# T products among the gate projections, and a state recurrence done by sums, a scan of every fourth step and an expansion

## The chip, the core and the metric

The kernel runs on one core of a Trainium2 chip. The metric is device time in microseconds of one execution, lower is better. The core has five engines with instruction streams of their own: TensorE (PE in the rows, PEld for its weight loads), VectorE (DVE), ScalarE (ACT), GpSimd (POOL) and SyncE (SP), which here issues nearly all DMAs.

## What is computed

Two transformer-like blocks on 512 tokens of width 1024. The first (two attentions, a cross attention and an MLP) is untouched. The second begins with the "even mixer", and the change lies in its S5 part, a bidirectional complex linear recurrence over 256 context and 512 latent tokens:

```python
lam_bar = jnp.exp(lam * step)
b_bar = ((lam_bar - 1.0) / lam)[..., None] * lax.complex(b_re, b_im)
bu = lax.complex(einsum('btgh,gph->btgp', u, b_bar.real), einsum('btgh,gph->btgp', u, b_bar.imag))
_, s = lax.associative_scan(_linear_recurrence, (a, bu), axis=1)      # s[t] = lam_bar * s[t-1] + bu[t]
return einsum('btgp,ghp->btgh', s.real, c_re) - einsum('btgp,ghp->btgh', s.imag, c_im)
```

with 48 groups of 16 channels and 64 states, forward and backward; `y = yf + yb + d * u`. Beside it, the mixer has a Fourier branch (256 channels), a gate projection `z`, a GLU and an output projection.

## The kernel before

**S5 in chunks.** Tokens are taken in chunks of eight, 32 context and 64 latent ones. `U[o]` (three tiles, 16 groups each) holds the inputs chunk by chunk. Three products on TensorE use them:
- the *state inputs*: 24 group pairs `gp`, each 8 products of `win` (fetched from the table `WinD` in DRAM, two pairs per tile) with `U` (L1209), evacuated into `St`, 128 partitions x 96 chunks x 2 directions x re/im x 24 pairs (L1213 on VectorE for odd pairs under 16, L1215 on ScalarE for the rest);
- the *T products*: what a chunk gives itself. `T` is fetched from `WD` by 8 DMAs a tile (L1263), the product of `T` and `U` (L1319) goes into `YC[o]`;
- the *E products*: `St` times `E` (fetched from `ED`, L1335; products L1343), added to `YC` by VectorE (L1348).

Between the first and the last, VectorE runs the recurrence over the 96 chunks: `tree` (L1184 to L1197) composes the first 32 chunks, the context, into one state by five levels of doubling, first for pairs 0 to 15, then for 16 to 23. The scan then goes chunk by chunk from 32 to 95, eight instructions a step on 128x48 elements (L1231 to L1237; four operations, two directions). The E products need the whole of it.

**What else runs there.** TensorE in the meantime does, in this order, the Fourier branch's input projection (`gemm_tok`, tiles `ub`), the gate projection `z` in four column groups of 256 (`gemm_ch`, 48 products of 128x512 each; the groups are called z3, z0, z1, z2 in the order in which they run), the transform (`k_dft`, then eight products with `fw`, result `yf`) and the Fourier part of the output projection (`even_out` below, 48 products of 128x512). Each matrix is used as a high and a low part: `wload` fetches `raw` (L131), ScalarE rounds it to `whi` (L137), VectorE subtracts to get `wlo` (L138, two instructions of 128x1024 for a z group). `mm3` (L175 to L177) issues hi x hi, lo x hi, hi x lo, so a group can't go on without its `wlo`. `raw`, `whi` and `wlo` have two buffers each.

**What sets the order.** Each engine runs its instructions in the order that the tile framework fixed when the program was built: it takes the instructions as written, with the place in the code as priority and its own model of their times, and gives buffers of the pools (`t4`: 12 of 4 KB, `big`: 9 of 8 KB, two PSUM banks `sc`, three `mm`) as they come free. `behind(n)` lowers a priority; the scan stands under `behind(3000)`. `self.step()`, called in the gemm helpers after the weights of a column group have been asked for, moves a generator in `self.sides` on; `self.after(n, f)` runs `f` after `n` flushes (one for each output tile). A matmul of type f32 (state inputs, T, E, `fw`) shows as two records in the trace.

Of the kernel before, what the change touches and what calls it, by code (L numbers as in the profile page):

```python
# [12 lines left out]
F32 = mybir.dt.float32  # L13
F32R = mybir.dt.float32r
AF = mybir.ActivationFunctionType
# [68 lines left out]
class Net:  # L84
# [8 lines left out]
    def setup(self):  # L93
        ctx, tc, nc, A = self.ctx, self.tc, self.nc, self.A
        P = lambda name, bufs, **k: ctx.enter_context(tc.tile_pool(name=name, bufs=bufs, **k))
        self.const = P("const", 1)
        self.sm = P("sm", 8)
        self.wp = P("wp", 2)
        self.t4 = P("t4", 12)
        self.big = P("big", 9)  # L100
        self.ps = P("ps", 1, space=PSUM)
        self.dram = P("dram", 1, space=bass.MemoryType.DRAM)
        self.ident = self.const.tile([128, 128], F32, name="ident")
        make_identity(nc, self.ident)
        self.mhalf = self.const.tile([128, 1], F32, name="mhalf")
        nc.vector.memset(self.mhalf, -0.5)
        self.sides = []
        self.late = []
# [795 lines left out]
    def s5_tables(self):  # L904

        nc, A = self.nc, self.A
        V = nc.vector
# [7 lines left out]
        ap = A["s5_log_step_2"]  # L915
# [40 lines left out]
        p = self.trp()  # L956
# [9 lines left out]
        t = self.ptile("pow")  # L966
# [24 lines left out]
        self.s5P = self.t4k("s5P")[:, :576].rearrange("p (j r n) -> p j r n", j=4, r=3)  # L991
        re, im = sw[:, 0], sw[:, 1]
        x = t[:, :48]
        for j in range(4):
# [170 lines left out]
    def even(self, hT, U, vpool):  # L1165
        nc, A = self.nc, self.A
        V = nc.vector
# [11 lines left out]
        def tree(g0, gn):  # L1179

            mt = [self.t4k("tree"), self.t4k("tree")]
            for lev in range(5):
                h = 1 << lev
                n = 16 // h  # L1184
                for d in range(2):
                    m1, m2 = mt[d][:, :4 * n * gn].rearrange("p (k m r g) -> k p m r g", k=2, m=n, r=2)
                    to = lambda t: t.to_broadcast([128, n, 2, gn])
                    if lev:
                        P3 = self.s5P[:, lev - 1, :, d * 24 + g0:d * 24 + g0 + gn]
                        a, b = to(P3[:, None, 0:1]), to(P3[:, None, 1:3])  # L1190
                    else:
                        a, b = [to(t[:, None, d, :, g0:g0 + gn]) for t in (self.s5A, self.s5B)]
                    dst = steps(d, 2 * h - 1, 2 * h, n, g0, gn, False)
                    V.tensor_mul(m1, a, steps(d, h - 1, 2 * h, n, g0, gn, False))
                    V.tensor_mul(m2, b, steps(d, h - 1, 2 * h, n, g0, gn, True))
                    V.tensor_add(m1, m1, dst)
                    V.tensor_add(dst, m1, m2)  # L1197

        for gp in range(24):
            o, l = divmod(gp, 8)  # L1200
            if gp % 2 == 0:
                win = self.t4k("win").rearrange("p (j d r n) -> p j d r n", j=2, d=2, r=2)
                nc.sync.dma_start(win, self.WinD[:, gp:gp + 2])
            p = self.bank("sc", 2)[:, :384].rearrange("p (r n) -> p r n", r=4)
            for d in range(2):
                for r in range(2):
                    for g in range(2):
                        u = 64 * (g ^ gp % 2)
                        nc.tensor.matmul(p[u:u + 64, 2 * d + r], win[:, gp % 2, d, r, 64 * g:64 * g + 64],  # L1209
                                         U[o][:, 8 * g + l, 32 * d:32 * d + 96], start=True, stop=True)  # L1210
            dst = St[:, :, :, :, gp].rearrange("p s d r -> p (d r) s")
            if gp % 2 and gp < 16:
                V.tensor_copy(dst, p)  # L1213
            else:
                nc.scalar.activation(dst, p, AF.Copy)  # L1215
        tree(0, 16)
        tree(16, 8)

        def at(d, j, swap=False):

# [4 lines left out]


        mt = self.const.tile([128, 192], F32, name="scan").rearrange("p (d m r g) -> d m p r g", d=2, m=2, r=2)
        with self.behind(3000):
            for j in range(32, 96):
                for d in range(2):  # L1230
                    V.tensor_mul(mt[d][0], self.s5A[:, d], at(d, j - 1))  # L1231
                for d in range(2):
                    V.tensor_mul(mt[d][1], self.s5B[:, d], at(d, j - 1, swap=True))  # L1233
                for d in range(2):
                    V.tensor_add(mt[d][0], mt[d][0], at(d, j))  # L1235
                for d in range(2):
                    V.tensor_add(at(d, j), mt[d][0], mt[d][1])  # L1237


        sz = [self.b8("sz", (128, 4, 512)) for _ in range(2)]  # L1240
# [16 lines left out]
        Ts = []  # L1257
        for o in range(3):
            T = self.b8("T", (128, 16, 128))
            for k in range(8):  # L1260
                src = bass.AP(tensor=self.WD.tensor, offset=self.WD.offset + o * 16 * 3840 + (7 - k) * 16,
                              ap=[[240, 16], [3840, 16], [1, 128]])
                nc.sync.dma_start(T[k * 16:(k + 1) * 16], src)  # L1263
            Ts.append(T)
# [17 lines left out]
        pq = []  # L1282
        for a, b in ((0, 258), (258, 514)):
            wh, wl = self.wload(A["k_dft"], 4, (a, b))
            t = self.t4k("pq")[:, :2 * (b - a)].rearrange("p (m n) -> p m n", m=2)
# [22 lines left out]
            self.split(*self.nat(t, yf[0][:, m], yf[1][:, m]))  # L1308


        YCs = []
        for o, T in enumerate(Ts):
            YCs.append(self.t4k("YC").rearrange("p (k l h) -> p k l h", k=8, h=16))
            for l0 in (0, 4):
                p = self.bank("sc", 2).rearrange("p (l n) -> p l n", l=4)
                for l in range(4):
                    for g in range(2):
                        k = 8 * g + l0 + l
                        nc.tensor.matmul(p[64 * g:64 * g + 64, l], U[o][:, k, 32:96], T[:, k], start=True, stop=True)  # L1319
                nc.scalar.activation(YCs[o][:, :, l0:l0 + 4].rearrange("p k l h -> p l k h"),  # L1320
                                     p.rearrange("p l (k h) -> p l k h", h=16), AF.Copy)

        gate = self.row(self.adaD[0, 2 * D:3 * D], self.t4k("gate"))

        self.gemm_tok([(yf[0][:, m], yf[1][:, m]) for m in range(2)], A["even_w_out_2"][0][768:], cols(0, D, 512), self.gated(gate))


        ga = []
        for o in range(3):
            YC = YCs[o]  # L1330
            for l0 in (0, 4):

                ps = [b[:, :256].rearrange("p (l n) -> p l n", l=2) for b in (self.bank("sc", 2), self.mm())]
                E = self.b8("E", (128, 4, 2, 2, 128))
                nc.sync.dma_start(E, self.ED[:, o * 8 + l0:o * 8 + l0 + 4])  # L1335
                for j0 in (0, 2):
                    for d in range(2):
                        s0 = 1 if d else 31
                        for r in range(2):
                            for j in (j0, j0 + 1):  # L1340
                                for g in range(2):
                                    q = slice(64 * (g ^ j % 2), 64 * (g ^ j % 2) + 64)
                                    nc.tensor.matmul(ps[j % 2][64 * g:64 * g + 64, j // 2], St[q, s0:s0 + 64, d, r, o * 8 + l0 + j], E[q, j, d, r],  # L1343
                                                     start=(d == 0 and r == 0), stop=(d == 1 and r == 1),
                                                     tile_position=(q.start, 64 * g), skip_group_check=True)
                for b, q in enumerate(ps):
                    dst = YC[:, :, l0 + b:l0 + 4:2].rearrange("p k l h -> p l k h")
                    V.tensor_add(dst, q.rearrange("p l (k h) -> p l k h", h=16), dst)  # L1348
# [171 lines left out]
```

## Time and profile before

| | |
|---|---|
| median of 3 runs | 1365.91 us (1364.2 to 1366.62) |
| the profiled execution | 1367.87 us, span from first to last instruction 1366.1 us |
| busy: PE, DVE, ACT, POOL | 95%, 72%, 41%, 5% |
| mean granted TensorE clock | 0.987 of full speed |
| DMA | 178.07 MB, mean 130 GB/s |

How to read it: times in the trace are microseconds from the span's start. A timeline row gives start, length, engine, line, operation, out<-in, shape, and in square brackets the idle time just before with what ended it. Instructions of an engine overlap at their ends, so what one costs in a row of them is the distance from start to start, not its length. The even mixer's S5 part, from the first state input to the GLU, runs from 969.5 to 1111.4 us.

### The profile page before, as it was taken

The page shows a single profiled execution, that of the slowest core. Times are in us where ns is not written, and L with a number is a line of the kernel's source. Part 1 is how long each engine was busy: PE and PEld are TensorE (multiplying, and loading weights), DVE is VectorE, ACT ScalarE, POOL GpSimd, SP SyncE. Part 2 cuts the span into 40 slices and gives each one's busy share as a digit, 9 for nine tenths or more (in the row PEclk, how much of TensorE's full clock was granted, in tenths as well). Part 3 has the DMA queues.
Part 4 walks back from the last instruction along what each step waited for, and adds up shares of the span by engine and source line. Part 5 has one row for each costly group of instructions (what it writes and reads, how often), then busy time and mean ns, then how long its engine had stood idle before and what let it go on. Part 6 is the DMA issues. An engine that isn't in the chain of part 4 may idle for free. (4 is left out here: it accounts for less than half of the span.)

```text
span 1366.1 us, 21191 instructions
## 1 busy us (share of the span) xinstructions
PE 1300.5 (95%) x8106; PEld 1081.4 (79%) x8106; DVE 987.5 (72%) x2284; ACT 557.6 (41%) x992; POOL 71.6 (5%) x135
## 2 busy tenths in 40 slices
PE   6999999999999999999999999979999789999997
PEld 5999577678888888787887887778888578787886
DVE  6998897868966464897999955683499966623545
ACT  5533643654526243433433433552433254333222
POOL 2000000021100010000000001010000000200000
PEclk9999999999999999999999999999999999999999
DMA  6422001155852236534777754541316934321321
GB/s 211 124 66 90 25 8 62 31 180 162 276 202 94 93 77 172 186 108 157 205 208 210 225 192 139 185 140 61 109 54 77 283 105 162 104 93 62 125 91 62
DMA packets 151877, 178.07 MB, mean 130 GB/s; under 512 B 27124, under 2 KB 118490, under 8 KB 151008
## 3 DMA queue, kind: packets, MB, share of 16 engines
q1 hardware_dynamic: 148560, 168.17, 40.6%
q0 software_dynamic: 3216, 8.56, 2.0%
q8 instruction: 64, 1.05, 0.3%
q14 instruction: 37, 0.30, 0.1%
HBM read 161.24 MB, written 15.45 MB: 129 GB/s over the span
## 5 line engine op out<-in xcount | busy, mean ns | idle before, releaser
L137 ACT ACTIVATE whi<-raw 128x1024 fp32r<-128x1024 f32 (+2 forms) x197 | 198.5, 1026 | 286.5 <-PE mm L176 114.3
L138 DVE TENSOR_TENSOR wlo<-raw,whi 128x1024 fp32r<-128x1024 f32 (+2 forms) x197 | 229.6, 1182 | 117.8 <-ACT whi L137 115.4
L175 PE MATMUL mm<-hmh,whi 128*128 128x512 f32 (+1 forms) x288 | 106.4, 369 | 0.0
L176 PE MATMUL mm<-hml,whi 128*128 128x512 f32 (+1 forms) x288 | 105.4, 366 | 0.0
L177 PE MATMUL mm<-hmh,wlo 128*128 128x512 f32 (+1 forms) x288 | 105.3, 366 | 0.0
L175 PE MATMUL mm<-whi,ah 128*128 128x512 f32 x256 | 101.8, 399 | 3.3 <-DVE x L620 3.3
L177 PE MATMUL mm<-whi,al 128*128 128x512 f32 x256 | 100.1, 394 | 0.2
L176 PE MATMUL mm<-wlo,ah 128*128 128x512 f32 x256 | 100.1, 393 | 0.0
L175 PE MATMUL mm<-whi,hTh 128*128 128x256 f32 (+1 forms) x304 | 88.5, 291 | 3.4 <-ACT whi L137 2.7
L176 PE MATMUL mm<-wlo,hTh 128*128 128x256 f32 (+1 forms) x304 | 86.9, 286 | 0.0
L177 PE MATMUL mm<-whi,hTl 128*128 128x256 f32 (+1 forms) x304 | 86.9, 286 | 0.0
L620 DVE TENSOR_TENSOR x<-mm,x 128x512 f32<-128x512 f32 x87 | 58.7, 685 | 32.6 <-PE mm L177 32.3
L781 DVE SCALAR_TENSOR_TENSOR adas<-adaw,cond,adas 128x1024 f32<-128x1024 f32 x56 | 70.6, 1277 | 10.2 <-DMA adaw<-ada_w_dram 10.0
L175 PE MATMUL mm<-h2h,whi 128*128 128x512 f32 x160 | 62.8, 392 | 0.0
L175 PEld LDWEIGHTS mm<-whi,ah 128*128 128x128 f32 x256 | 48.3, 189 | 18.1 <-DVE x L620 5.6
L175 PEld LDWEIGHTS mm<-whi,hTh 128*128 128x128 f32 x304 | 58.8, 193 | 4.4 <-ACT whi L137 3.1
L177 PE MATMUL mm<-h2h,wlo 128*128 128x512 f32 x160 | 62.3, 389 | 0.0
L176 PE MATMUL mm<-h2l,whi 128*128 128x512 f32 x160 | 62.3, 389 | 0.0
L175 PEld LDWEIGHTS mm<-hmh,whi 128*128 128x128 f32 x288 | 54.3, 189 | 9.6 <-issue 1.0
L177 PEld LDWEIGHTS mm<-hmh,wlo 128*128 128x128 f32 x288 | 54.3, 189 | 8.8
L176 PEld LDWEIGHTS mm<-hml,whi 128*128 128x128 f32 x288 | 54.4, 189 | 8.4
L176 PEld LDWEIGHTS mm<-wlo,hTh 128*128 128x128 f32 x304 | 58.5, 193 | 1.4 <-issue 1.3
(515 smaller groups left out, 3296.5 us busy)
## 6 DMA issues: line engine op xcount, KB each, us to landing
adaw<-ada_w_dram SPq DMA_DIRECT2D x48, 512.0 KB
raw<-w_up_dram SPq DMA_DIRECT2D x16, 1024.0 KB
raw<-w_down_dram SPq DMA_DIRECT2D x16, 1024.0 KB
raw<-odd_w_in_dram SPq DMA_DIRECT2D x12, 1024.0 KB
raw<-w_in_dram SPq DMA_DIRECT2D x11, 1024.0 KB
raw<-w_kv_cross_dram SPq DMA_DIRECT2D x8, 1024.0 KB
raw<-even_w_in_dram SPq DMA_DIRECT2D x8, 1024.0 KB
WinD<-wst SPq DMA_DIRECT2D x24, 256.0 KB
```

The costliest lines, as they stand in the source:

```text
L137: nc.scalar.activation(hi[:, k], raw[:, k], AF.Copy)
L138: nc.vector.tensor_sub(lo[:, k], raw[:, k], hi[:, k].bitcast(F32))
L175: nc.tensor.matmul(out, lh, rh, start=(first and i == 0), stop=False)
L176: nc.tensor.matmul(out, lh, rl, start=False, stop=False)
L177: nc.tensor.matmul(out, ll, rh, start=False, stop=(final and i == n - 1))
L620: self.nc.vector.tensor_add(self.x[i][:, c:c + n], p, self.x[i][:, c:c + n])
L781: nc.vector.scalar_tensor_tensor(acc[v], w, cond[:, v, k:k + 1], acc[v], op0=OP.mult, op1=OP.add)
```

## The change

- The state inputs' tiles `win` are fetched up to four ahead; evacuations all go to ScalarE; the products take banks of `sc` and `mm` in turn.
- The recurrence is done in other steps. `join(lev, j0, n, ...)` does one level: chunk j0, j0+2h, ... gets the state of h chunks before it. `join(0, 1, 48)` (384 elements an instruction) runs after every four pairs, `join(1, 3, 24)` (384 elements) after every eight, over all 96 chunks. The scan goes over every fourth chunk, 7 to 95, with the fourth power of lambda. Then chunks 33, 37, ... (`join(1, 33, 16)`, 256 elements) and 32, 34, ... (`join(0, 32, 32)`, 512 elements) are expanded for 8 pairs at a time.
- Scan and expansion are a generator in `self.sides`, moved on by `self.step()`; `behind(3000)` is gone. A `step` is added in the transform.
- T tiles 0 and 1 are fetched right after the tables, T2 within the scan; their products run by `self.after` among the projections. The six `E` tiles are fetched earlier: three at the scan's end, three after z.
- `s5P` (powers) goes from four levels in `t4` to two in `const`; `t4` has 13 buffers; the DMA scratch is set to 8192.

```diff
+        jt = [self.t4k("join") for _ in range(2)]
+        def join(lev, j0, n, g0, gn):
+            h = 1 << lev
+            for d in range(2):
+                m1, m2 = jt[d][:, :4 * n * gn].rearrange("p (k m r g) -> k p m r g", k=2, m=n, r=2)
...
+                dst = steps(d, j0, 2 * h, n, g0, gn, False)
+                V.tensor_mul(m1, a, steps(d, j0 - h, 2 * h, n, g0, gn, False))
+                V.tensor_mul(m2, b, steps(d, j0 - h, 2 * h, n, g0, gn, True))
+                V.tensor_add(m1, m1, dst)
+                V.tensor_add(dst, m1, m2)
...
+                while len(wins) < min(gp // 2 + 4, 12):
+                    wins.append(self.t4k("win").rearrange("p (j d r n) -> p j d r n", j=2, d=2, r=2))
...
-            if gp % 2 and gp < 16:
-                V.tensor_copy(dst, p)
-            else:
-                nc.scalar.activation(dst, p, AF.Copy)
-        tree(0, 16)
-        tree(16, 8)
+            nc.scalar.activation(dst, p, AF.Copy)
+
+            if gp % 4 == 3:
+                join(0, 1, 48, gp - 3, 4)
+            if l == 7:
+                join(1, 3, 24, gp - 7, 8)
+        Ts += [t_load(o) for o in range(2)]
+        for o in range(3):
+            self.after(2 + 3 * o, lambda o=o: t_part(o))
...
-        with self.behind(3000):
-            for j in range(32, 96):
+        def scan():
+            for j in range(7, 96, 4):
                 for d in range(2):
-                    V.tensor_mul(mt[d][0], self.s5A[:, d], at(d, j - 1))
+                    V.tensor_mul(mt[d][0], A4[d][:, 0:1].to_broadcast([128, 2, 24]), at(d, j - 4))
...
+                if j == 39:
+                    Ts.append(t_load(2))
+                if j == 95:
+                    Es.extend(e_load(n) for n in range(3))
+                if j % 28 == 11:
+                    yield
+            for g0 in (0, 8, 16):
+                join(1, 33, 16, g0, 8)
+                join(0, 32, 32, g0, 8)
+                yield
+        self.sides.append(scan())
```

How the fixed orders change, at three places. VectorE, where the low part of z1's weights is made. Before (`wlo_10454` is z1's, two halves of it):

```order
L1237 TENSOR_TENSOR St<-scan 128x48 x2
L1231 TENSOR_TENSOR scan<-s5A,St 128x48 x2
L1233 TENSOR_TENSOR scan<-s5B,St 128x48 x2
L138 TENSOR_TENSOR wlo_10454<-raw_10452,whi_10453 128x1024
L1235 TENSOR_TENSOR scan<-scan,St 128x48 x2
L1237 TENSOR_TENSOR St<-scan 128x48
L138 TENSOR_TENSOR wlo_10454<-raw_10452,whi_10453 128x1024
L1237 TENSOR_TENSOR St<-scan 128x48
L1231 TENSOR_TENSOR scan<-s5A,St 128x48 x2
```

and in the changed kernel (`wlo_10140` is z1's, `wlo_10262` z2's, `wlo_10360` the transform's):

```order
L1193 TENSOR_TENSOR join_9333<-s5A,St 128x512
L1196 TENSOR_TENSOR St<-join_9334 128x16x2x8
L1194 TENSOR_TENSOR join_9333<-s5B,St 128x512
L1195 TENSOR_TENSOR join_9333<-join_9333,St 128x512
L1193 TENSOR_TENSOR join_9334<-s5A,St 128x512
L1196 TENSOR_TENSOR St<-join_9333 128x32x2x8
L1194 TENSOR_TENSOR join_9334<-s5B,St 128x512
L1195 TENSOR_TENSOR join_9334<-join_9334,St 128x512
L1196 TENSOR_TENSOR St<-join_9334 128x32x2x8
L138 TENSOR_TENSOR wlo_10140<-raw_10138,whi_10139 128x1024 x2
L138 TENSOR_TENSOR wlo_10262<-raw_10260,whi_10261 128x1024 x2
L138 TENSOR_TENSOR wlo_10360<-raw_10358,whi_10359 128x774
```

The split of z1's weights stood in the middle of the scan; now it stands behind the last instruction of the expansion. In the same stream, the split of z0 (`wlo_10003`) stands behind the 9th of the 23 scan steps and the four `ub` splits, that of z3 ahead of the first join.

TensorE, end of z0 and begin of z1 in the changed kernel (`mm_10091` is z0's last tile, `sc_10117` and `sc_10127` the T2 products, `mm_10208` and `mm_10234` z1's first two tiles):

```order
L176 MATMUL mm_10091<-hll_8439,whi_10002 128x512
L177 MATMUL mm_10091<-hlh_8438,wlo_10003 128x512
L1223 MATMUL sc_10117<-T_9919,U_8656 64x128 x8
L1223 MATMUL sc_10127<-T_9919,U_8656 64x128 x8
L175 MATMUL mm_10208<-hlh_8436,whi_10139 128x512
L176 MATMUL mm_10208<-hll_8437,whi_10139 128x512
L175 MATMUL mm_10234<-hlh_8436,whi_10139 128x512
L176 MATMUL mm_10234<-hll_8437,whi_10139 128x512
L177 MATMUL mm_10208<-hlh_8436,wlo_10140 128x512
```

The T products, which stood in the output projection, now stand in the input projection, in z0 and between z0 and z1; the fifth product of z1 needs `wlo_10140`.

SyncE in the changed kernel (`raw_10138` and `raw_10260` are z1's and z2's weights):

```order
L1232 DMA win_9565<-WinD 128x1024
L1203 DMA T_9671<-WD 16x16x128 x3
L1203 DMA T_9680<-WD 16x16x128 x8
L1203 DMA T_9919<-WD 16x16x128 x8
L131 DMA raw_10138<-even_w_in_dram 128x8x256
L1208 DMA E_10202<-ED 128x2048
L1208 DMA E_10204<-ED 128x2048
L1208 DMA E_10206<-ED 128x2048
L131 DMA raw_10260<-even_w_in_dram 128x8x256
```

Before, both came ahead of all T and E tiles. Now z1's are queued behind the T tiles, and z2's behind the first three E tiles.

## Rows read from the trace of the kernel before

**Rows 1.** The page's head and its busy times.
```profile
span 1366.1 us, 21191 instructions
PE 1300.5 (95%) x8106; PEld 1081.4 (79%) x8106; DVE 987.5 (72%) x2284; ACT 557.6 (41%) x992; POOL 71.6 (5%) x135
```
**Rows 2.** Stretches: length, busy PE, PEld, DVE, ACT, POOL; PEclk, DMA share, GB/s.
```profile
1003.60:1047.30 43.70, 43.70 (x196) 36.19 (x195) 43.70 (x304) 12.94 (x19) 3.04 (x6) 1.00 0.27 72
1061.40:1090.60 29.20, 22.11 (x176) 18.18 (x176) 28.80 (x159) 6.39 (x12) 0.00 (x0) 0.88 1.11 293
```
**Rows 3.** Timeline of PE: last product of `ub`, first of z3, first after z2.
```profile
1003.61 0.28 PE L177 MATMUL mm<-whi,hll 128*128 128x256 f32 x1
1003.73 0.40 PE L175 MATMUL mm<-hlh,whi 128*128 128x512 f32 x1
...
1047.28 1.05 PE L1277 MATMUL tr<-fw 128*128 128x128 f32 x8
```
**Rows 4.** Timeline of PE from the transform to the E products: the idle times.
```profile
1052.31 0.38 PE L176 MATMUL mm<-wlo,ub 128*128 128x256 f32 x1 [0.98 <-DVE wlo L138]
...
1061.45 0.50 PE L175 MATMUL mm<-whi,yf 128*128 128x512 f32 x1 [2.66 <-ACT yf L309]
...
1067.39 3.76 PE L1319 MATMUL sc<-T,U 128*64 128x128 f32 x64
1076.37 3.32 PE L1319 MATMUL sc<-T,U 128*64 128x128 f32 x32 [5.22 <-DMA raw<-even_w_out_dram]
1080.81 2.06 PE L1343 MATMUL sc<-E,St 64*64 64x128 f32 x32 [1.12 <-DVE St L1237]
...
1090.60 1.73 PE L1343 MATMUL mm<-E,St 64*64 64x128 f32 x26
```
**Rows 5.** Timeline of PE and of ACT in the E products.
```profile
1097.15 0.40 PE L1343 MATMUL sc<-E,St 64*64 64x128 f32 x2 [1.07 <-issue]
...
1110.32 1.11 PE L1356 MATMUL tr<-ident,YC 128*128 128x128 f32 x4 [3.69 <-ACT ga L1357]
...
1108.72 1.06 ACT L137 ACTIVATE whi<-raw 128x1024 fp32r<-128x1024 f32 x1 [6.25 <-DMA raw<-odd_w_in_dram]
```
**Rows 6.** Timeline of DVE in the tree: 512 and 256 elements, start to start.
```profile
986.41 0.69 DVE L1194 TENSOR_TENSOR tree<-s5A,St 128x512 f32<-128x512 f32 x1
987.02 0.69 DVE L1195 TENSOR_TENSOR tree<-s5B,St 128x512 f32<-128x512 f32 x1
...
998.45 0.41 DVE L1194 TENSOR_TENSOR tree<-s5A,St 128x256 f32<-128x256 f32 x1
998.78 0.41 DVE L1197 TENSOR_TENSOR St<-tree 128x256 f32<-128x256 f32 x1
```
**Rows 7.** Timeline of DVE in the scan: the first operation of two steps.
```profile
1076.91 0.33 DVE L1231 TENSOR_TENSOR scan<-s5A,St 128x48 f32<-128x48 f32 x2
...
1077.87 0.33 DVE L1231 TENSOR_TENSOR scan<-s5A,St 128x48 f32<-128x48 f32 x2
```
**Rows 8.** Timeline of DVE: a weight split, a split of ub, a weight split.
```profile
1005.82 1.22 DVE L138 TENSOR_TENSOR wlo<-raw,whi 128x1024 fp32r<-128x1024 f32 x1
1006.96 0.42 DVE L310 TENSOR_TENSOR ub<-ubf,ub 128x256 fp32r<-128x256 f32 x1
1007.29 1.22 DVE L138 TENSOR_TENSOR wlo<-raw,whi 128x1024 fp32r<-128x1024 f32 x1
```
**Rows 9.** Timeline of ACT and DVE: evacuations of state inputs.
```profile
973.11 0.87 ACT L1215 ACTIVATE St<-sc 128x384 f32<-128x384 f32 x1
...
989.15 4.59 ACT L1215 ACTIVATE St<-sc 128x384 f32<-128x384 f32 x5 [0.16 <-PE sc L1209]
...
976.51 0.82 DVE L1213 COPY St<-sc 128x384 f32<-128x384 f32 x1 [0.98 <-PE sc L1209]
```
**Rows 10.** Timeline of PE after an idle time: first and fourteenth product.
```profile
912.46 0.55 PE L175 MATMUL mm<-whi,cxh 128*128 128x256 f32 x1 [6.47 <-DVE UC L815]
...
915.36 0.28 PE L176 MATMUL mm<-wlo,cxh 128*128 128x256 f32 x1
```

More of the change, by code (lines that the diff above doesn't have):

```diff
@@ L98, in setup @@
         self.wp = P("wp", 2)
-        self.t4 = P("t4", 12)
+        self.t4 = P("t4", 13)
         self.big = P("big", 9)
@@ L989, in s5_tables @@
         V.tensor_copy(self.s5B[:, :, 1], l8[:, 1])
-        self.s5P = self.t4k("s5P")[:, :576].rearrange("p (j r n) -> p j r n", j=4, r=3)
+        self.s5P = self.const.tile([128, 288], F32, name="s5P").rearrange("p (j r n) -> p j r n", j=2, r=3)
         re, im = sw[:, 0], sw[:, 1]
         x = t[:, :48]
-        for j in range(4):
+        for j in range(2):
             a, b, c = (self.s5P[:, j, k] for k in range(3))
@@ L1177, in steps @@
             return bass.AP(tensor=fl.tensor, offset=fl.offset + a + (24 if swap else 0), ap=ap)
[L1179 to L1190, printed above, removed]
-                    else:
[L1192 to L1197, printed above, removed]
+        jt = [self.t4k("join") for _ in range(2)]
@@ new lines, in join @@
+        def join(lev, j0, n, g0, gn):
+            h = 1 << lev
+            for d in range(2):
+                m1, m2 = jt[d][:, :4 * n * gn].rearrange("p (k m r g) -> k p m r g", k=2, m=n, r=2)
+                to = lambda t: t.to_broadcast([128, n, 2, gn])
+                if lev:
+                    P3 = self.s5P[:, lev - 1, :, d * 24 + g0:d * 24 + g0 + gn]
+                    a, b = to(P3[:, None, 0:1]), to(P3[:, None, 1:3])
+                else:
+                    a, b = [to(t[:, None, d, :, g0:g0 + gn]) for t in (self.s5A, self.s5B)]
+                dst = steps(d, j0, 2 * h, n, g0, gn, False)
[3 more added lines that the diff above has]
+                V.tensor_add(dst, m1, m2)
@@ new lines, in t_load, with e_load @@
+        def t_load(o):
+            T = self.b8("T", (128, 16, 128))
+            for k in range(8):
+                src = bass.AP(tensor=self.WD.tensor, offset=self.WD.offset + o * 16 * 3840 + (7 - k) * 16,
+                              ap=[[240, 16], [3840, 16], [1, 128]])
+                nc.sync.dma_start(T[k * 16:(k + 1) * 16], src)
+            return T
+        def e_load(n):
+            E = self.b8("E", (128, 4, 2, 2, 128))
+            nc.sync.dma_start(E, self.ED[:, 4 * n:4 * n + 4])
+            return E
@@ new lines, in even, with t_part @@
+        Ts, Es = [], []
+        YCs = [None] * 3
+        wins = []
+        def t_part(o):
+            YCs[o] = self.t4k("YC").rearrange("p (k l h) -> p k l h", k=8, h=16)
+            for l0 in (0, 4):
+                p = self.bank("sc", 2).rearrange("p (l n) -> p l n", l=4)
+                for l in range(4):
+                    for g in range(2):
+                        k = 8 * g + l0 + l
+                        nc.tensor.matmul(p[64 * g:64 * g + 64, l], U[o][:, k, 32:96], Ts[o][:, k], start=True, stop=True)
+                nc.scalar.activation(YCs[o][:, :, l0:l0 + 4].rearrange("p k l h -> p l k h"),
+                                     p.rearrange("p l (k h) -> p l k h", h=16), AF.Copy)
@@ L1201, in even @@
             if gp % 2 == 0:
-                win = self.t4k("win").rearrange("p (j d r n) -> p j d r n", j=2, d=2, r=2)
-                nc.sync.dma_start(win, self.WinD[:, gp:gp + 2])
-            p = self.bank("sc", 2)[:, :384].rearrange("p (r n) -> p r n", r=4)
+                while len(wins) < min(gp // 2 + 4, 12):
+                    wins.append(self.t4k("win").rearrange("p (j d r n) -> p j d r n", j=2, d=2, r=2))
+                    nc.sync.dma_start(wins[-1], self.WinD[:, 2 * len(wins) - 2:2 * len(wins)])
+                win = wins[gp // 2]
+            p = (self.mm() if gp % 2 else self.bank("sc", 2))[:, :384].rearrange("p (r n) -> p r n", r=4)
             for d in range(2):
@@ L1227, in even @@
         mt = self.const.tile([128, 192], F32, name="scan").rearrange("p (d m r g) -> d m p r g", d=2, m=2, r=2)
-        with self.behind(3000):
-            for j in range(32, 96):
+        A4 = [self.s5P[:, 1, :, d * 24:d * 24 + 24] for d in range(2)]
+        def scan():
+            for j in range(7, 96, 4):
                 for d in range(2):
-                    V.tensor_mul(mt[d][0], self.s5A[:, d], at(d, j - 1))
+                    V.tensor_mul(mt[d][0], A4[d][:, 0:1].to_broadcast([128, 2, 24]), at(d, j - 4))
                 for d in range(2):
-                    V.tensor_mul(mt[d][1], self.s5B[:, d], at(d, j - 1, swap=True))
+                    V.tensor_mul(mt[d][1], A4[d][:, 1:3], at(d, j - 4, swap=True))
                 for d in range(2):
@@ L1256, in even @@
         self.gemm_ch(hT, W, zc[3:] + zc[:3], e_z)
[L1257 to L1264, printed above, removed]
+        Es.extend(e_load(n) for n in range(3, 6))
         yf = [self.t4.tile([128, 2, 512], F32R, tag="t4", name=self.nm("yf")) for _ in range(2)]
@@ L1284, in even @@
             wh, wl = self.wload(A["k_dft"], 4, (a, b))
+            self.step()
             t = self.t4k("pq")[:, :2 * (b - a)].rearrange("p (m n) -> p m n", m=2)
@@ L1308, in even @@
             self.split(*self.nat(t, yf[0][:, m], yf[1][:, m]))
[L1311 to L1321, printed above, removed]
         gate = self.row(self.adaD[0, 2 * D:3 * D], self.t4k("gate"))
         self.gemm_tok([(yf[0][:, m], yf[1][:, m]) for m in range(2)], A["even_w_out_2"][0][768:], cols(0, D, 512), self.gated(gate))
+        for _ in self.sides.pop():
+            pass
         ga = []
@@ L1333, in even @@
                 ps = [b[:, :256].rearrange("p (l n) -> p l n", l=2) for b in (self.bank("sc", 2), self.mm())]
-                E = self.b8("E", (128, 4, 2, 2, 128))
-                nc.sync.dma_start(E, self.ED[:, o * 8 + l0:o * 8 + l0 + 4])
+                E = Es[o * 2 + l0 // 4]
                 for j0 in (0, 2):
@@ L1511 @@
     arrays.update(shape_constants())
-    nc = bacc.Bacc("TRN2", target_bir_lowering=False, num_devices=1)
+    nc = bacc.Bacc("TRN2", target_bir_lowering=False, num_devices=1, dynamic_dma_scratch_size=8192)
     A = {n: nc.dram_tensor(n + "_dram", list(a.shape), mybir.dt.from_np(a.dtype), kind="ExternalInput").ap()
```

1 line of the change is left out of this document (removed).

## The prediction

> **What bounds the kernel now.** I read the page first. TensorE is busy for 95% of a span of 1366.1 us, VectorE for 72% [rows 1], so VectorE's work costs time only where TensorE waits for it. I then cut the S5 part into stretches [rows 2]. From 1003.6 to 1047.3 both engines are busy throughout: TensorE runs the four z groups without a gap, and VectorE's scan runs beside them. From 1061.4 to 1090.6 TensorE is busy for 22.1 of 29.2 us at a mean granted clock of 0.88, VectorE for 28.8. Last came TensorE's timeline, to see what each gap waits for [rows 4]: 0.98 us for a weight split, 2.66 for `yf`, 5.22 in the T products, where a DMA landed last, and 1.12 for the end of the scan. The E products begin in earnest at 1090.60, and two gaps follow there, of 1.07 and 3.69 us, the second behind a ScalarE stuck on a weight DMA [rows 5]. These are what the change can win. All z groups together take 1047.28 - 1003.73 = 43.55 us [rows 3], 10.89 each and 0.227 a product, so z1 starts at 1003.73 + 2 x 10.89 = 1025.5.
>
> **VectorE's work, old and new.** Start to start, an instruction takes 0.61 us for 512 elements and 0.33 for 256 [rows 6], so 0.47 for 384 by interpolation; a scan step takes 0.96 [rows 7]; a weight split 1.14 and a `ub` split 0.33 [rows 8].
> - Removed: 64 steps x 0.96 = 61.4, the two trees (986.4 to about 1005, some 18), and eight evacuations.
> - Added: joins of levels 0 and 1, 6 + 3 calls x 8 x 0.47 = 33.8; 23 steps x 0.96 = 22.1; the expansion, 3 x 8 x (0.33 + 0.61) = 22.6. Together 78.5.
>
> So VectorE's total hardly falls. What changes is the order: z1's weight split, which stood in the middle of the scan, now stands behind all of this. I add up the stream:
> - First join: z3's rounding goes on the ScalarE stream until 973.11, then three more evacuations at 0.84 each [rows 9]: 975.6. Later ones come at most 0.92 apart (five in 4.59 us), 3.7 for four pairs, while VectorE needs 5.6 on average for four (nine calls for six fours), so VectorE sets the pace.
> - Joins until 975.6 + 33.8 = 1009.4.
> - Nine steps and four `ub` splits, 8.6 + 1.3: z0's split starts at 1019.3; its first half is there at 1020.5, the pair done at 1021.6.
> - Fourteen steps, 13.4: 1035.0. Expansion, 22.6: 1057.6. First half of z1's split, 1.14: **1058.7**. z2's follows at 1059.9.
>
> **What TensorE does meanwhile.** The 24 pairs of state inputs, started at 969.5 and at most 0.92 apart [rows 9], end by 991.6. The input projection follows, 96 products x 0.12 [rows 3] = 11.5, with T0 in it (3.76 / 2 = 1.88 a T product [rows 4]): 1005.0. z3 is held back some 3 us more, since the `ub` evacuations that free its banks now stand behind z0's rounding on ScalarE; it ends near 1019, and z0 waits for its split until 1020.5. z0, T1 and T2 (10.9 + 2 x 1.88) end near 1035.2. After four products of z1 it stands idle until 1058.7, some 23 us. That is 33.2 us after z1's old start.
>
> From there to the end of `even_out`, where E products used to begin at 1090.60:
> - z1, 44 products left x 0.227: 10.0, and 1.3 because the engine was idle: after a gap of 6.47 us [rows 10] thirteen products took 915.36 - 912.46 = 2.90 us where thirteen at full clock take 1.56 (0.12 each). 1070.0.
> - `fw` and nine E products (0.8 + 1.2), z2 10.9: 1082.9.
> - Transform and its eight products: 1061.45 - 2.66 - 0.98 - 1047.28 - 0.8 = 9.7: 1092.6.
> - `yf`: the chain over VectorE and ScalarE remains without the scan between; I take 1.2 of the 2.66: 1093.8.
> - `even_out`, 48 x 0.227 = 10.9, and the first bank's last E products, 0.9: 1105.6.
>
> That is **15.0 us late**. Three further items are in it already at zero: the T products' wait (5.22) and its slow clock, and the wait for the scan.
>
> **The E products.** With all E tiles loaded by then and the last weights queued behind them asked for earlier relative to this stage, I expect both gaps to close: -4.8, which leaves **+10**. The bounds are all of it, which I take, and nothing, if the same ScalarE wait returns: +15.
>
> Costs that I set at zero: z1's weights, now queued behind eight T2 loads that wait for the T0 product near 1001, are there by about 1020 at the old pace of 0.9 us a load; VectorE's order covers them until 1058. If the order were better, they would matter from 1035 on. z2's, behind two E tiles that wait for the T2 product (1035), have 24 us. The two removed levels of powers are ten 128x48 instructions under the MLP. Small shifts of order before 969 I put at +-1.
>
> **One price not in the trace:** joins of level 0 work on runs of four elements; those in the rows had runs of eight or sixteen, and both cost the same. An evacuation, which writes single elements, takes 0.82 us for 384 [rows 9] where a contiguous instruction would take about 0.55. So each of the 48 instructions costs between 0 and 0.27 more, 0 to +13 us in all; I take 0, nearer to the runs of eight. [...]
>
> **The rivals.**
> - *The stalls removed outweigh the late split* (faster, 7%). T wait, scan wait and E gaps sum to 12 us and go for certain. For: VectorE is released from a serial tail. Against: they are counted above. It decides if z1's split comes by 1058.7 - 10 = 1048.7, that is, if VectorE's 82 us from 975.6 are done in 72. A 384-element instruction would have to take 0.33, the row of 256. If VectorE did all of it in 67, the result would be 1361.
> - *Runs of four are slow* (11%): +13 on top, 1389.
> - *The E stage wins nothing* (14%): +15, 1381.
> - *The change does not move the T products out of the way* (3%): if T2's loads come so late that T2, which stands ahead of z1 on TensorE, is what waits. They would have to land after 1057, 45 us after their turn; nothing in the DMA share of 0.27 in that stretch [rows 2] suggests so. Up to that point the time stays 1376.
> - *It cancels out* (4%): z1's split near 1049, 1366.
>
> **The numbers.** The sum is made against a profiled execution of 1367.87 us with a span of 1366.1; the median of the three runs is 1365.91. 1365.9 + 10 = **1376**. Chance for the forecast itself, within 4 us, 61%. The range goes down to 1369, which is the E gaps, the `yf` wait and 2 us of the front in its favour, and up to 1388, nearly the whole price of slow runs. About 0.2% (2.7 us) is what a measurement here can tell from no change: faster 7%, same 4%, slower 89%.
>
> **What would show it.** In the new trace: joins of 384 at 0.47 start to start; the last expansion near 1057; one gap of over 20 us on TensorE ended by VectorE's L138 in z1, with products at half clock behind it; no gap at the T products or at the scan's end; the stretch up to the E products 15 us later than 1090.6. It is wrong if that gap is under 12 us, or if joins take another time than 0.47, or if more than 5 us come from before 969.

## The result, and the profile after

The changed kernel takes 1380.66 us (median of 4, 1377.37 to 1382.86), the kernel before beside it 1366.26 (median of 4, 1364.20 to 1367.11). The ratio is 1.0113, 95% interval 1.0099 to 1.0127: slower by over 1%, where 1376 (1369 to 1388) was forecast. The profiled executions stand 10.7 us apart in span (1376.8 against 1366.1), 10.8 in time (1378.71 against 1367.87). In two of the kernels below, rank_t2_last and old_t2_last, one execution ran at a granted clock of 0.56 and 0.65 and took 2135 and 1834 us; it is left out of their medians and ratios.

The page's head and busy times of the changed kernel, beside [rows 1]:

```profile
span 1376.8 us, 20867 instructions
PE 1298.7 (94%) x8106; PEld 1079.9 (78%) x8106; DVE 979.5 (71%) x1978; ACT 559.7 (41%) x1000; POOL 71.9 (5%) x135
```

VectorE has lost 306 instructions and only 8.0 us. The stretches, with the columns of [rows 2]:

```profile
1003.00:1035.50 32.50, 30.20 (x164) 23.79 (x164) 32.50 (x207) 9.07 (x16) 3.04 (x6) 0.91 0.37 86
1035.50:1057.20 21.70, 0.09 (x2) 0.04 (x1) 21.66 (x44) 0.24 (x1) 0.00 (x0) 0.59 0.36 137
1057.20:1071.00 13.80, 13.80 (x52) 11.23 (x52) 1.05 (x1) 1.25 (x3) 0.00 (x0) 0.78 0.15 39
1071.00:1107.00 36.00, 35.27 (x194) 28.45 (x193) 18.89 (x24) 14.66 (x27) 0.57 (x1) 1.00 0.55 190
```

For 21.7 us TensorE does nothing while VectorE is busy throughout; behind it the granted clock is 0.78; from 1071 on hardly a wait is left. TensorE's timeline, the counterpart of [rows 3 to 5]:

```profile
1002.94 0.79 PE L175 MATMUL mm<-hlh,whi 128*128 128x512 f32 x1 [3.34 <-ACT ubf L1298]
...
1018.81 0.50 PE L177 MATMUL mm<-hlh,wlo 128*128 128x512 f32 x1 [1.53 <-DVE wlo L138]
...
1034.36 0.50 PE L175 MATMUL mm<-hlh,whi 128*128 128x512 f32 x1 [0.77 <-ACT whi L137]
...
1057.16 0.79 PE L177 MATMUL mm<-hlh,wlo 128*128 128x512 f32 x1 [21.61 <-DVE wlo L138]
1057.76 0.63 PE L175 MATMUL mm<-hlh,whi 128*128 128x512 f32 x1
...
1063.30 0.41 PE L176 MATMUL mm<-hll,whi 128*128 128x512 f32 x1
...
1093.96 0.50 PE L175 MATMUL mm<-whi,yf 128*128 128x512 f32 x1 [0.28 <-ACT yf L309]
...
1106.98 0.38 PE L1373 MATMUL mm<-E,St 64*64 64x128 f32 x2
...
1112.90 0.39 PE L1373 MATMUL sc<-E,St 64*64 64x128 f32 x2 [0.22 <-DVE YC L1378]
```

The 1.12 us for the end of the scan, the 5.22 at the T products and the gaps of 1.07 and 3.69 in the E products [rows 4, 5] are gone. In their place stands one gap of 21.61 us in z1. VectorE's timeline there (joins, z0's split, first and last of the expansion, z1's split):

```profile
973.72 0.56 DVE L1193 TENSOR_TENSOR join<-s5A,St 128x384 f32<-128x384 f32 x1 [0.88 <-ACT St L1242]
974.20 0.55 DVE L1194 TENSOR_TENSOR join<-s5B,St 128x384 f32<-128x384 f32 x1
...
1007.13 0.55 DVE L1196 TENSOR_TENSOR St<-join 128x384 f32<-128x384 f32 x1
...
1017.54 2.35 DVE L138 TENSOR_TENSOR wlo<-raw,whi 128x1024 fp32r<-128x1024 f32 x2
...
1033.28 0.42 DVE L1193 TENSOR_TENSOR join<-s5P,St 128x256 f32<-128x256 f32 x1
...
1055.28 0.69 DVE L1196 TENSOR_TENSOR St<-join 128x512 f32<-128x512 f32 x1
1055.89 2.35 DVE L138 TENSOR_TENSOR wlo<-raw,whi 128x1024 fp32r<-128x1024 f32 x2
```

And SP's queue, which asks for the weights (`raw`; the one at 999.82 is z1's, the one at 1034.87 z2's):

```profile
976.56 23.16 SPq L1203 DMA_DIRECT2D T<-WD  x19
999.82 0.40 SPq L131 DMA_DIRECT2D raw<-even_w_in_dram  x1
1021.95 12.52 SPq L1208 DMA_DIRECT2D E<-ED  x3
1034.87 0.38 SPq L131 DMA_DIRECT2D raw<-even_w_in_dram  x1
```

z1's weights are asked for behind the last T2 load; the T2 loads wait for the T0 product, which frees their buffer. The prediction named the place of z1's split and that its weights are queued behind the T tiles; whether the one follows from the other was left open. The experiments ask that.

### The profile page after: what moved, and what is told of

Its sections match the earlier page's. It is cut to its first block, busy times and chain, and to the rows that moved or that the text cites. A ratio compares the mean times of both kernels' runs of the same rounds, so it can differ in the third digit from the quotient of the medians.

```text
span 1376.8 us, 20867 instructions
## 1 busy us (share of the span) xinstructions
PE 1298.7 (94%) x8106; PEld 1079.9 (78%) x8106; DVE 979.5 (71%) x1978; ACT 559.7 (41%) x1000; POOL 71.9 (5%) x135
## 4 chain that ended last, share of the span: by engine, by line
PE 70%; DVE 18%; ACT 4%; issue 3%; DMA 2%; POOL 1%; SPq 0%; DVEq 0%; POOLq 0%; ACTq 0%
PE mm L175 18%; PE mm L177 18%; PE mm L176 18%; DVE wlo L138 2%; PE pv L601 2%; PE tr L586 1%; DVE m L539 1%; PE sc L573 1%; PE sc L577 1%; DMA raw<-w_in_dram 1%; DVE acc L540 1%; ACT whi L137 1%; DVE join L1195 1%; DVE join L1193 1%; DVE St L1196 1%
## 5 line engine op out<-in xcount | busy, mean ns | idle before, releaser
L137 ACT ACTIVATE whi<-raw 128x1024 fp32r<-128x1024 f32 (+2 forms) x197 | 198.4, 1026 | 263.5 <-PE mm L176 110.1
```

Of the source, the lines that this page charges most:

```text
L137: nc.scalar.activation(hi[:, k], raw[:, k], AF.Copy)
```

## The experiments

Executions of the same code differ ahead of the part that was changed: the first state input starts between 967.5 and 972.6 us in the traces. So the table also gives the *tail*, the span less the start of the first state input, for the one profiled execution of each. The kernel before ran beside each group of runs, with medians from 1364.4 to 1366.3; so between groups the ratios compare better than the medians.

| kernel | recurrence | T2's loads, and E | median | ratio to before (95%) | tail |
|---|---|---|---|---|---|
| before | old | after z, late | 1366.26 | 1 | 396.6 |
| after | new | ahead of z1's weights | 1380.66 | 1.0113 (1.0099 to 1.0127) | 408.8 |
| after_again | new | same | 1378.04 | 1.0103 (1.0088 to 1.0117) | 407.4 |
| rank_only | new, low priority | same | 1381.65 | 1.0112 (1.0094 to 1.0131) | 408.7 |
| t_only | old | same | 1376.56 | 1.0088 (1.0071 to 1.0105) | 405.5 |
| rec_only | new | as before | 1374.23 | 1.0065 (1.0048 to 1.0082) | 403.7 |
| no_expand | new, no expansion | ahead of z1's weights | 1356.04 | 0.9938 (0.9924 to 0.9951) | 384.6 |
| t2_late | new | T2 behind z's weights | 1366.77 | 1.0015 (1.0006 to 1.0024) | 396.7 |
| e_after | new | T2 behind z's, E behind transform's | 1360.15 | 0.9965 (0.9953 to 0.9977) | 389.6 |
| t2_last | new | T2 behind transform's, then E | 1358.69 | 0.9955 (0.9943 to 0.9967) | 389.2 |
| rank_t2_last | new, low priority | same | 1360.23 | 0.9954 (0.9941 to 0.9967) | - |
| t2_last_pool | new | same | 1359.97 | 0.9969 (0.9958 to 0.9980) | 389.5 |
| old_t2_last | old | same | 1366.12 | 1.0012 (0.9999 to 1.0026) | 393.8 |
| old_t2_late | old | T2 behind z's, E behind transform's | 1369.75 | 1.0043 (1.0027 to 1.0059) | 401.3 |

**no_expand: is it the expansion that z1 waits for?**

```diff
-                join(1, 33, 16, g0, 8)
-                join(0, 32, 32, g0, 8)
```

> The changed kernel with the expansion left out (48 VectorE instructions, 22.6 us; three of four chunks then lack their full state, so this is only for the time). z1's split stands behind the scan as before, and the queue of loads is as it was. My theory (the gap is the expansion standing ahead of the split): z1's first half is there near 1035.5, the gap of 21.61 us shrinks to 0.5 to 2 us and the slow clock behind it goes; z2 may wait a few us for its weights, which are asked for at 1034.87 behind three E tiles: 1357 to 1363. Rival C (z1's or z2's weights come too late anyway, and the expansion only covers that): a gap of 10 us or more stays in z1 or z2, 1368 or more. An expansion that costs only its own time where nothing waits for it would give 1378 to 1381.

1356.04, 1 us under the range of my theory and 12 under the rivals. The gap is down to the rounding's 0.77 us; TensorE's row in place of 1034.36 and 1057.16:

```profile
1036.47 0.50 PE L175 MATMUL mm<-hlh,whi 128*128 128x512 f32 x1 [0.77 <-ACT whi L137]
```

Of the tail, 408.8 - 384.6 = 24.2 us are gone, for 22.6 us of VectorE's work and the slow clock behind the gap: z1's weights were there, only their split stood too far back. z2's came in time as well.

**t_only and rec_only: which half of the change puts it there?** t_only takes the kernel after and puts `tree`, the 64-step scan under `behind(3000)` and four levels of powers back. rec_only does the reverse:

```diff
-        Ts += [t_load(o) for o in range(2)]
-        for o in range(3):
-            self.after(2 + 3 * o, lambda o=o: t_part(o))
...
-                if j == 39:
-                    Ts.append(t_load(2))
-                if j == 95:
-                    Es.extend(e_load(n) for n in range(3))
...
-        Es.extend(e_load(n) for n in range(3, 6))
+        Ts += [t_load(o) for o in range(3)]
...
+        for o in range(3):
+            t_part(o)
...
-                E = Es[o * 2 + l0 // 4]
+                E = e_load(o * 2 + l0 // 4)
```

> The other half: T and E tiles fetched early and T products among the projections, as changed, while tree, 64-step scan and its low priority are as before. T2's eight DMAs stand ahead of z1's weights, and in the fixed order z1's split stands at 80% of the scan's rows (in the kernel before at 14%). My theory: z1's split is there only near 1059, a gap of 20 to 25 us in z1 as in the changed kernel though no expansion exists here, and the whole is 1379 to 1386. If the new recurrence were the cause of the late split, this kernel would have the T wait and the E gaps won and nothing lost: 1350 to 1358.

> One half of the change: the new recurrence (joins, scan of every fourth chunk, expansion, state inputs evacuated by ScalarE), while T and E tiles are fetched and their products done where the kernel before did. z1's split then stands at 70% of the scan's rows and z2's in the expansion's first part. My theory: no long gap in z; the T wait (5.22), its slow clock and the E gaps (1.07 and 3.69) are there again, the wait for the end of the scan (1.12) is gone since the recurrence ends near 1062, z3 is still held some 3 us by the later evacuations: 1363 to 1368, no change against the kernel before. If the recurrence itself were what costs the 14 us: 1376 to 1382.

t_only has the gap with no expansion in it, in TensorE's timeline:

```profile
1053.26 0.80 PE L177 MATMUL mm<-hlh,wlo 128*128 128x512 f32 x1 [26.01 <-DVE wlo L138]
```

26.0 us, 1.0 over the upper end; its total of 1376.56 is below mine, since scan and z1's split came 6 us earlier than I had added up. So the long gap does not need the new recurrence. rec_only has no such gap, as expected, but is 1374.23, not 1363 to 1368. TensorE's waits there:

```profile
982.86 1.55 PE L1239 MATMUL sc<-U,win 128*64 128x96 f32 x16 [3.75 <-DMA win<-WinD]
...
1062.76 0.38 PE L176 MATMUL mm<-wlo,ub 128*128 128x256 f32 x1 [4.42 <-DVE wlo L138]
...
1081.79 1.97 PE L1223 MATMUL sc<-T,U 128*64 128x128 f32 x32 [0.88 <-DMA raw<-even_w_out_dram]
1086.22 2.68 PE L1368 MATMUL sc<-E,St 64*64 64x128 f32 x32 [2.46 <-DMA E<-ED]
...
1116.87 1.12 PE L1381 MATMUL tr<-ident,YC 128*128 128x128 f32 x4 [4.05 <-ACT ga L1382]
```

The T and E waits are back, as I had it. Two I had not counted: state inputs that wait for a table tile (SP asks for z1's weights ahead of it) and the transform's second split, now behind the expansion (4.42 where it was 0.98). Neither half alone is faster than the kernel before. Both keep the new fetching and evacuation of the state inputs; no run takes those back by themselves.

**t2_late: T2's loads behind z's weights.**

```diff
-            self.after(2 + 3 * o, lambda o=o: t_part(o))
+            self.after((2, 5, 10)[o], lambda o=o: t_part(o))
...
-                if j == 39:
+                if j == 71:
                     Ts.append(t_load(2))
```

> The changed kernel with one load moved: the eight DMAs of T2 are asked for two steps later, behind z1's and z2's weights on SP's queue, and the T2 product follows later with them. Nothing else in the source differs. In the order that is fixed at build time z1's split then stands within the scan (at some 88% of its rows) and z2's within the expansion, no longer behind it. My theory (the 21.6 us come from where z1's split stands, and it stands there because z1's weights are queued behind T2's eight DMAs): z1's split is there near 1031.5, TensorE goes from z0 to z1 without a stop, the 21.61 us, the 2.8 us of slow clock behind them and the 0.77 us go, and a wait of 1 to 4 us for VectorE comes at the transform's split, behind the expansion: 1380.7 - 23 = 1357, between 1354 and 1362. Rival A (it is the recurrence's work itself that holds TensorE up, wherever the split stands): the wait comes back in z2 or in the E products, 1372 or more. Rival B (T2 now comes too late and its product is waited for): a gap at the T products, 1362 to 1368.

The gap in z1 is gone, and so is the 0.77: its trace shows no wait of TensorE between 1020.06 and the T2 product at 1056.2. But 1366.77 is some 10 us more than my theory had. It lies in the range of rival B, yet T2's product is not waited for, so that rival's reason is out. Some 1.4 us was lost just behind the wait for z0's split (2.87 us here, 1.53 in the changed kernel): from 1018 to 1026 the granted clock was 0.79, and T1's product took 3.4 us in place of 2.0. Most of the rest went into the E products themselves. In this order all those for PSUM bank `sc` stand ahead of the transform, those for `mm` behind the output projection. The E products alone, TensorE's stretches of t2_late (busy PE, PEld; PEclk, DMA share, GB/s), for `sc` and for `mm`:

```profile
1061.80:1069.30 7.50, 7.43 (x128) 7.24 (x128) 1.00 1.01 399
...
1096.40:1102.20 5.80, 5.80 (x104) 5.80 (x106) 1.00 0.00 0
```

The same of the changed kernel, where the two banks alternate from 1108.4 on (the first 22 records are all of `mm`):

```profile
1107.00:1112.60 5.60, 5.60 (x162) 5.49 (x162) 1.00 0.04 7
```

58 and 56 ns a record against 35, the second with no DMA at all beside it. 384 records at 57 are 21.9 us, at 35 13.4: an estimate of 8.5 us. (From 1108.4 to 1112.2 alone it is 3.80 us for 138 records, some 28 ns.)

**rank_only: or is it the lost priority?**

```diff
-        def scan():
+        with self.behind(3000):
...
-        self.sides.append(scan())
+        self.sides.append(loads())
```

(`loads` keeps the T2 and E loads where they were.)

> The changed kernel with the low priority of the kernel before given to scan and expansion again (both written at once under behind(3000)), while every load stands where the change put it, T2's eight DMAs ahead of z1's weights. In the fixed order z0's split now stands ahead of the scan, but z1's and z2's still stand behind the whole expansion. My theory (the queue of loads decides where the split is planned, not the priority): a gap of 20 to 27 us in z1 again, 1377 to 1383. If the missing priority were the cause: no long gap, 1355 to 1360.

1381.65, with this row on TensorE:

```profile
1061.64 0.80 PE L177 MATMUL mm<-hlh,wlo 128*128 128x512 f32 x1 [23.57 <-DVE wlo L138]
```

Priority alone moves z0's split (its 1.53 us are gone), not z1's. Together with t2_late this shows that the place of T2's loads decides it. That the framework's own model holds z1's weights for late, and so fills VectorE with the expansion first, is what these orders suggest; no run shows the model's times.

**e_after and t2_last: the rest of it.**

```diff
                 if j == 71:
                     Ts.append(t_load(2))
-                if j == 95:
-                    Es.extend(e_load(n) for n in range(3))
...
+                if g0 == 16:
+                    Es.extend(e_load(n) for n in range(3))
...
-        Es.extend(e_load(n) for n in range(3, 6))
...
         for _ in self.sides.pop():
             pass
+        Es.extend(e_load(n) for n in range(3, 6))
```

This is e_after against t2_late. In t2_last the T2 load stands at `g0 == 16` instead, and ahead of the output projection come `Es.extend(e_load(n) for n in range(3))` and `t_part(2)`.

> The kernel of the run with T2 behind the z weights, with the six E tiles now asked for behind the transform's weights (three) and behind the output projection's (three). In that run the long gap was gone but only 14 us came back; there the products of E had moved ahead of the transform, all of one PSUM bank first (128 records in 7.46 us, 58 ns each) and those of the other bank after the output projection, where the changed kernel alternates between the two (162 records in 5.70 us, 35 ns each). In the order of this kernel they alternate again for five of six groups. If the lost alternation is what took the rest: 8 to 10 us less than that run, near 1358 (1354 to 1362), with some 4 us of waiting left at the transform's split, which still stands behind the expansion. If something else took it: 1364 to 1368.

> T2's eight DMAs go behind the transform's weights too, and the T2 product ahead of the output projection; E tiles behind that. In the fixed order z1's split stands at 88% of the scan, z2's a fifth into the expansion and the transform's first in its second half. My theory: no wait over 5 us on TensorE between z0 and the E products; even_out ends some 23 us earlier than the 1106.98 of the changed kernel: 1355, between 1351 and 1360, faster than the kernel before. If T2 or E, asked for so late, are waited for (as in the run of the recurrence alone, 3.5 and 2.5 us): 1360 to 1366.

1360.15: 1.0015 - 0.9965 = 0.5%, 6.8 us, come back with the alternation, in the tail 7.1. That is a balance: some 1.4 us of it is T1's slow clock, which this run does not have, and against it the transform's first split is waited for 5.05 us where t2_late had 0.66. So the reading of t2_late fits, in size too, but no run changes the alternation alone. t2_last has with 1358.69 the lowest median of the kernels with the whole computation in them, 0.45% under the kernel before and within the noise of e_after; it is 4 us over my middle. What remains is a wait of 3.34 us for `ubf` ahead of z3, one of 1.82 for z0's split, and one that I had at 4 us, for the transform's second split behind the expansion:

```profile
1062.99 0.58 PE L176 MATMUL mm<-wlo,ub 128*128 128x256 f32 x1 [4.82 <-DVE wlo L138]
```

**rank_t2_last** adds the low priority to t2_last and puts the four `ubf` blocks in one tile (`t = ubf[:, i, :n]`).

> As the run with T2 behind the transform's weights, and besides scan and expansion at low priority, so that z0's split goes ahead of the scan, and the four ubf blocks in one tile, so that their evacuations go ahead of z0's rounding on ScalarE. The two waits of the changed kernel ahead of z0 (3.34 for ubf with some 2.9 us of slow clock behind it, 1.53 for z0's split) should go. But z1's split still comes after some 88% of the scan, near 1031, and TensorE then waits there instead: within 3 us of the run without these two edits. If TensorE's own work were what sets the end there: 6 to 8 us less.

The ratio is that of t2_last: no gain, as expected. That the waits ahead of z0 went and moved to z1 is not shown: the one profiled execution is that of 2135 us.

**old_t2_last and old_t2_late: is the new recurrence worth anything?** Both are t_only with the loads moved, as in t2_last and e_after (T2 product between z and transform).

> The recurrence of the kernel before (tree, scan of 64 steps at low priority), and the loads of the run in which T2 stands behind the transform's weights: T0 and T1 early with their products among the projections, T2's product ahead of the output projection, E behind. In the fixed order z1's split stands at 35% of the scan's rows, z2's at 37%, the transform's at 52% and 69%. My theory (the place of the splits decides, and the recurrence's own form hardly matters as long as it fills VectorE's gaps): no wait over 3 us on TensorE in z, the scan ends near 1074 and is waited for 1 to 2 us by the E products: 1346 (1342 to 1353), faster than with the new recurrence (1358.7), since a scan at low priority lets every split through. If the new recurrence is what makes the early E products possible: the end of the scan is waited for 10 us or more, 1356 to 1364.

> As that run, with T2's eight DMAs two steps earlier, ahead of the transform's weights but behind z2's. The transform's split then stands at 80% of the scan in place of 52%. My theory: no wait in z, one of some 5 us at the transform (behind VectorE's scan, as z1's was in the run with the early loads alone), 1351 (1347 to 1356). If T2's place mattered only for z1: the same as the other run within 1 us.

Both wrong by some 20 us. z is free of long waits, but TensorE waits further down, in old_t2_last:

```profile
1066.12 1.22 PE L175 MATMUL mm<-whi,yf 128*128 128x512 f32 x2 [5.32 <-ACT whi L137]
1073.39 0.80 PE L176 MATMUL mm<-wlo,yf 128*128 128x512 f32 x1 [6.04 <-DVE wlo L138]
...
1090.81 0.50 PE L1366 MATMUL sc<-E,St 64*64 64x128 f32 x2 [5.14 <-issue]
```

The output projection's split stands behind most of the scan, and its evacuations (sixteen instructions from 1075.9 on) ahead of the last steps, which end at 1091.8, not at 1074 (for the 5.14 us ahead of the E products the profile names no releaser). old_t2_late has 7.14 at the transform's split besides. So with T2 at the same place the new recurrence is faster, by 7.4 us in the medians (1358.69 against 1366.12) and 4.6 in the tails; for old_t2_late against e_after it is 9.6 and 11.7. It does shorten the stretch, which my expectation had denied.

**t2_last_pool: the last wait.** `wload` gets an engine, and the transform's second split goes to GpSimd: `eng=nc.gpsimd if a else None`.

> The run with T2 behind the transform's weights (1358.7), with one instruction moved: the second split of the transform, which stood behind the expansion on VectorE and was waited for 4.82 us by TensorE (until 1062.99), goes to GpSimd, which has nothing else to do there. Its rounding on ScalarE ends at 1055.1 in that run, TensorE needs the result at 1058.2. No row shows GpSimd subtracting 128x1024; writing as much takes it 0.95 us. My theory (that wait is on the path to the end): with a split of up to 3 us the wait goes, with 5 us half of it: 1354 to 1357. If GpSimd needs 8 us or more, or VectorE runs slower beside it: 1359 to 1363. If the wait were covered by what follows (the E products, VectorE's yf chain): 1358 to 1359.

No gain, 1359.97, as in the rival of a split of some 8 us or a slower VectorE. The wait only changed its cause, so whether it is on the path to the end is still not shown. GpSimd's, VectorE's and TensorE's rows:

```profile
1055.54 7.25 POOL L138 TENSOR_TENSOR wlo<-raw,whi 128x1024 fp32r<-128x1024 f32 x1 [40.60 <-PE tr L1314]
...
1059.92 0.68 DVE L1195 TENSOR_TENSOR join<-join,St 128x512 f32<-128x512 f32 x1
1060.63 2.71 DVE L1196 TENSOR_TENSOR St<-join 128x512 f32<-128x512 f32 x1
...
1062.85 0.45 PE L176 MATMUL mm<-wlo,ub 128*128 128x256 f32 x1 [4.37 <-POOL wlo L138]
```

**after_again** is the changed kernel itself, beside these.

> The changed kernel once more, beside these. From the first state input to the end it took 1376.8 - 968.0 = 408.8 us in its profile, the kernel before 1366.1 - 969.5 = 396.6, and the run with the low priority 408.7; the first state input itself came between 967.6 and 972.6 in nine profiles of code that is the same up to there. So I expect 408 to 409.5 again, and a median between 1377 and 1383. If the spread of the changed kernel's times came from its own part: another value by 2 us or more.

A tail of 407.4, just under what I expected, with a gap of 19.24 us in z1; 1378.04. Two executions of the same code differ by 1.4 us in the tail and by 0.5 in what lies ahead of it.

## Why the prediction was right, and where it was off

**VectorE's stream** came out as added up. Up to the restart of z1 all of it lies 1.5 to 1.9 us ahead, since the first state input started at 968.01, not 969.5:

| | forecast | measured |
|---|---|---|
| first join | 975.6 | 973.72 |
| joins end | 1009.4 | 1007.6 |
| scan ends, expansion starts | 1035.0 | 1033.28 |
| expansion ends | 1057.6 | 1055.9 |
| z1 goes on | 1058.7 | 1057.16 |
| gap | some 23 | 21.61 |
| z1 ends | 1070.0 | 1070.15 |
| even_out ends | 1105.6 | 1106.98 |

**Runs of four** cost nothing: joins go 0.48 us start to start (973.72, 974.20) where 0.47 was interpolated from runs of eight and sixteen [rows 6]. The rival at 1389 is out.

**The E stage** won what I took, and 0.9 more: from the end of even_out to the end of the span 1376.8 - 1106.98 = 269.8, before 1366.1 - 1090.60 = 275.5, that is 5.7 against 4.8 forecast. rec_only, without the early E loads, has gaps of 2.46 and 4.05 there; t_only, with them, none over 0.7.

**The slow clock** was the term that I mis-sized. I took 1.3 us from a gap of 6.47 [rows 10]. Fourteen products from 1057.16 to 1063.30 took 6.14 us, at 0.43 each, where fourteen at 0.227 take 3.18: 3.0 us. The granted clock was 0.50 from 1057.20 to 1063.30 and 1.00 from there to 1071.00, in the whole stretch 0.78.

**The front** was set at +-1 and came 1.5 us in favour. Without it the profiled execution would have shown +12.2 rather than +10.7. Of the 2.2 over the forecast, 1.7 are the slow clock and 1.2 even_out, which took 1106.98 - 1093.96 = 13.0 with the first E products in it where I had 11.8; the E stage gives 0.9 back. That the span hit the forecast within a microsecond is partly luck: the early front hid two terms that were too small.

**The medians** lie 14.4 us apart, in the second comparison 13.3 (1378.04 against 1364.79), the profiles 10.7. The front differs by up to 5 us between executions of the same code, and the profiled run of before (1367.87) is above its median. What is left of the difference is not settled.

**The rivals** fell as weighed: VectorE needed 82.2 us from 973.72 to 1055.9 where 82 were forecast, so the split could not come by 1048.7; T2's product was waited for by nobody. Two sums there were off without changing a choice: the stalls removed sum to 11.1 us, not 12, and the lower end of the range, 1369, counts the E gaps a second time; without them the items named for it reach down to about 1373.

## What to carry to other kernels

In a program whose order is fixed when it is built, a load asked for early can cost more than the wait that it removes: here the weights queued behind it were split late, and the engine that others waited for did other work first, though the weights were there. So move a load together with what it is moved past, and read where the short, waited-for instructions now stand on the busy engine. When a stall disappears and only part of it comes back, look at the work that has moved into the gap: its rate can be another there, here some 28 ns a record where two PSUM banks alternated and 57 with one bank at a time.

## What the runs showed of the hardware

- **Products on 64x64 tiles.** Where two PSUM banks alternate, the E products took some 28 ns a record of 128 columns (changed kernel, 138 records in 3.80 us from 1108.4 to 1112.2); one bank at a time, 56 to 58 (t2_late). In the code the products of one bank have two `tile_position` values, those of both banks together four. The products of 512 columns run at 0.227 us, which is 57 ns for 128 columns. So by this estimate a record took as long as 128 columns of such a product where one bank was used at a time, and half as long where two alternated. Bank and tile positions change together here, so which of the two decides is not shown.
- **GpSimd beside VectorE.** A subtraction of 128x1024 took GpSimd 7.25 us in t2_last_pool, VectorE 1.22 [rows 8]. VectorE was busy without a break for its first 5 us; then one VectorE instruction took 2.71 in place of 0.68 and ended 0.55 behind it. How much of the 7.25 is a wait, and what held the VectorE instruction, is not shown: no run here has GpSimd doing this alone.
- **The clock behind a gap.** Behind an idle time of 21.61 us TensorE's granted clock was 0.50 for 6.1 us (changed kernel, fourteen products in 6.14 us), behind one of 6.47 [rows 10] it was 0.50 for 2.90 us (kernel before, 912.46 to 915.36), and 1.00 right after each. In t_only fourteen products took 6.13 us behind an idle time of 26.01.
